# A two-layer float32 decoder trunk on one core: a re-priced instruction plan, float32r attention values, the last residual in halves, and ten matmuls on zeros ahead of TensorE's queue

## The chip, the cores and the metric

The kernel runs on one core of a Trainium2 chip. A core has TensorE (matmul, with a separate row for its weight loads), VectorE (DVE in the profile), ScalarE (ACT), GpSimd (POOL), and SyncE (SP), whose queue issues the DMA transfers here. The engines run their own queues in order and wait for each other by semaphores. The metric is the device time of one execution in microseconds (us), as the median of several runs.

## The reference

The input is 256 tokens of width 2048, in float32. Layer 0 mixes the tokens in two ways at once, with one input projection: sliding-window attention (16 query heads of 64, 2 key and value heads, blocks of 128 tokens, a learned sink for each head) and a gated delta rule (8 heads of 128). Layer 1 is a gated position mixing. Each layer ends with a SwiGLU feed-forward part of width 5632, and all residuals are added in float32.

```python
def reference(x, ...):
    h = x
    for i in range(DEPTH):
        j = i // 2
        if i % 2 == 0:
            h = h + even_mixer(rms_norm(h, even_norm[j]), ...)
        else:
            h = h + odd_mixer(rms_norm(h, odd_norm[j]), ...)
        h = h + swiglu(rms_norm(h, ffn_norm[i]), ...)
    return rms_norm(h, final_norm)
```

Inside the attention, for each block of 128 queries: scores against the block's own and the previous block's keys, a softmax with the sink, and then `einsum('bnhgqk,bnkhd->bnqhgd', p / denom, vb)`. The last product is what is called the value matmuls below.

## The kernel before

**Tiling.** The 256 tokens are two tiles of 128 rows (index t). A dense product runs over chunks of 512 output columns; `dense` (line 488) takes the input in blocks of 128 rows for each chunk. A weight tile `raw` holds four such blocks and comes by one DMA (1 MB, or 544 KB for the first chunk, which is only 272 wide). ScalarE casts each block to float32r (`whi`), VectorE subtracts to get the rest (`wlo`), and TensorE does three float32r matmuls for each token tile: activation-high by weight-high, activation-high by weight-low, activation-low by weight-high. There are three `raw` tiles, six `whi`, six `wlo` and four output banks `mm`. Activations are held as such high and low pairs in `unit` tiles, of which there are 58. `split` (line 446) makes a pair: a copy on ScalarE that casts, and a subtraction on VectorE.

**The first chunk.** `run` (line 1056) loads x in eight pieces `h` (four column chunks by two token tiles). `fill_unit` (line 452) transposes a piece on TensorE (four transposes into a `side` bank), multiplies by the norm's gain on VectorE, and splits. `chunk_stats` squares the piece on ScalarE with a running sum (its output goes to `junk`). The first product is the chunk "kvg" of the even mixer: keys, values and gates. The next is "qa0", the queries of the first eight heads.

**Small products.** Products other than the dense ones go to `side` banks: transposes, the delta rule's small products in float32 (a float32 matmul is two records in the profile), and products with the constant tiles `same` (line 723, `delta_inverse`) and `one` (line 587, `decay`) in float32r. In `delta_inverse`, each output is a pair of matmuls: the first operand is made by VectorE, the second by GpSimd.

**Attention.** `attention` (line 855) is called for two groups of heads and two token tiles. It transposes the probabilities (`tok_major`), copies each transposed block `pT` out on ScalarE, and multiplies by the values `va`: twelve float32 matmuls of 512 columns, each into one half of the output's rows. The result is split.

**The end.** `project` with `gain=None` writes the last dense product. In its last chunk `dense` holds back the second token tile's products by `LAG = 10`, so that the first tile finishes earlier. `residual` adds the product to `h`; then the square's sum, then h times the final gain `gf`. `finish` (line 1044) calls `end_norm` (a sum of four partial sums, a scale, and a power of -0.5 on GpSimd), scales the four pieces of a tile (three on VectorE, one on ScalarE) and writes them out.

**The order of work.** No instruction is issued as the program reads. Every operation is recorded (`Engine`, line 277 on) with a price in ns, a priority and its tile uses. `Schedule.plan` (line 190) then walks a clock: it takes at each step the engine that is free first and its ready operation of lowest priority number, gives it a tile if one is free, and sets its end by its price. `hop` (line 182) adds the way from engine to engine; to TensorE it is 1000 ns. The list sorted by planned start is the order in which each engine's queue is filled. A price in the table of `record` (lines 288 to 306) thus moves instructions everywhere, and on the chip the queues then keep that order whatever happens. In the profile all of them have line 179.

Of the kernel before, what the change touches and what calls it, by code (L numbers as in the profile page):

```python
# [16 lines left out]
P = 128  # L17
# [259 lines left out]
class Engine:  # L277
# [5 lines left out]
    def __getattr__(self, name):  # L283
        f = getattr(self.engine, name)

        def record(*args, **kw):
# [6 lines left out]
            elif k == "pe":  # L293
                cost = 3.0 + (107.0 if name == "transpose" else
                              (1.0 if aps[1].dtype == F32R and n >= 256 else 4.0) * n / 2.4)
# [6 lines left out]
            elif k == "dve":  # L302
                n = size(aps[1]) if name in ("tensor_reduce", "bn_stats") else n
                cost = (183.0 if name == "transpose" else 69.0) + (0.521 if name == "tensor_scalar" else 1.042) * n + 60.0 * scalars
            else:
                cost = 165.0 * n + 320.0 if ALU.pow in args else 1.9 * n + 200.0
# [9 lines left out]
class Trunk:  # L316
# [68 lines left out]
    def load_consts(self):  # L385
        nc, t = self.nc, self.t
        self.ident = self.keep((P, P), "ident")
        nc.sync.dma_start(self.ident, t["ident"])
        self.gains = self.const(t["gains"], [P, 4, 16], "gains")
        self.junk = self.keep((P, CW), "junk", BF16)  # L390
        self.mhalf = self.keep((P, 8), "mhalf")
        nc.vector.memset(self.mhalf, -0.5)
        self.phalf = self.keep((P, 8), "phalf")
        nc.vector.memset(self.phalf, 0.5)

# [134 lines left out]
    def project(self, w, units, gain, pcs=None):  # L530
# [3 lines left out]
        for n in range(NCH):  # L534
            self.residual(n, self.dense(w, units, n * size, pcs=pcs, lag=LAG if gain is None and n == NCH - 1 else 0))
            with self.prio(1):
# [7 lines left out]
                if gain is None:  # L544
                    for t in range(NT):
                        self.nc.vector.tensor_tensor(self.h[t][n], self.h[t][n], self.gf[n], ALU.mult)

# [286 lines left out]
    def attn_kv(self, ps):  # L834

        nc = self.nc
        self.va = self.small([P, NT, A_KV], "va")
        kk = self.unit(shape=(P, NT, 2, 2, 64))
        for t in range(NT):
# [3 lines left out]
            nc.scalar.activation(self.va[:, t], ps[t][:, A_KV:2 * A_KV], AF.Identity, scale=self.rstd[t])  # L843
        return kk

# [9 lines left out]
    def attention(self, kv, t, q, pair, kT):  # L855
# [35 lines left out]
        for s in ss:  # L891
            for b in range(nb):
                pT = self.unit()
                nc.scalar.copy(pT, self.tok_major(lambda m: s[:, m, b]))
                pTs.append(pT)
        out = self.side(P, 4, P)
        for r in range(2):
            rows = slice(64 * r, 64 * r + 64)
            for b, (own, kb) in enumerate(blocks):
                nc.tensor.matmul(out[rows].rearrange("p m i -> p (m i)"), self.va[:, kb, 64 * kv:64 * kv + 64],  # L900
                                 pTs[r * nb + b].rearrange("p m i -> p (m i)"), start=(b == 0), stop=(b == nb - 1))
# [142 lines left out]
    def finish(self):  # L1044
        nc = self.nc
        self.end_norm()
# [126 lines left out]
```

## Time and profile before

| | |
|---|---|
| time, median of 3 runs | 2168.47 us (2168.4 to 2168.81) |
| the profiled execution's own time | 2168.62 us |
| its span, first to last instruction | 2166.9 us |
| instructions | 27246 |
| mean granted TensorE clock | 0.999 |
| mean DMA rate | 184 GB/s, 399.08 MB moved |
| ACT table loads | 8 of 1283 ns |

The profiled execution's time is its span and 1.7 us around it. A row of a timeline gives the start of a group of like instructions from the span's start and how long it lasted, then the engine, the operation, what it writes and reads, the shape and the count; in brackets stands how long the engine had been idle and what ended that. `PEld` is TensorE's weight load, which overlaps its matmuls. A matmul's own length in the profile (some 390 ns at 512 columns) is longer than the distance to the next one's start, because matmuls are pipelined: distances of starts are what counts. In a table of windows, each row is a stretch of time with the busy time of each engine in the order of the head line, the granted clock, the DMA engines' share, and GB/s.

### The profile page before, as it was taken

How to read it: one execution, taken by the hardware profiler on the slowest of the kernel's cores; microseconds unless marked ns; L12 is line 12 of the kernel's file. 1: busy time of each engine (PE TensorE's matmuls, PEld its weight loads, DVE VectorE, ACT ScalarE, POOL GpSimd, SP SyncE). 2: the span in 40 equal slices, each digit the busy share in tenths (PEclk: the TensorE clock that was granted, in tenths of full speed). 3: DMA queues.
4: the chain of work that ended last, by engine and by line, in shares of the span. 5: the costliest groups of instructions: out<-in, count | busy, mean ns of one | idle time of the engine just before them, and what ended most of it. 6: DMA issues, size and time to landing. Idle time of an engine off the chain costs nothing.

```text
span 2166.9 us, 27246 instructions
## 1 busy us (share of the span) xinstructions
PE 2145.5 (99%) x9860; PEld 1774.7 (82%) x9860; DVE 1483.9 (68%) x2681; ACT 1133.6 (52%) x2034; POOL 55.7 (3%) x68
## 2 busy tenths in 40 slices
PE   8999999999999999999999999999999999999998
PEld 7788888888888888888888888888888888888886
DVE  7796786667766776657775576666677667755563
ACT  7665655554554555445545545555455544544453
POOL 1010110000000000000010000000000000000000
PEclk9999999999999999999999999999999999999999
DMA  7442434555555555556565555555555555555553
GB/s 246 136 156 79 156 117 156 194 179 193 194 195 194 192 194 194 194 194 201 204 231 184 194 171 178 189 188 192 193 190 194 194 193 194 195 202 194 194 199 131
DMA packets 58455, 399.08 MB, mean 184 GB/s; under 512 B 6976, under 2 KB 7232, under 8 KB 11216
## 3 DMA queue, kind: packets, MB, share of 16 engines
q1 hardware_dynamic: 57168, 393.61, 53.5%
q0 software_dynamic: 1152, 3.74, 0.6%
q8 instruction: 77, 1.26, 0.2%
q14 instruction: 58, 0.48, 0.1%
HBM read 395.22 MB, written 2.10 MB: 183 GB/s over the span
## 4 chain that ended last, share of the span: by engine, by line
PE 96%; DVE 2%; DMA 1%; issue 1%; ACT 1%; SPq 0%; POOL 0%; POOLq 0%; DVEq 0%; ACTq 0%
PE mm L179 90%; PE side L179 5%; DVE unit L179 1%; DVE wlo L179 1%; DMA raw<-in_even_in 1%; DMA h<-in_x 0%; ACT junk L179 0%; ACT whi L179 0%; DVE uc L179 0%; SPq L179 0%; DVE yt L179 0%; DVE yr L179 0%; DVE h L179 0%; POOL unit L179 0%; ACT L179 0%
## 5 line engine op out<-in xcount | busy, mean ns | idle before, releaser
L179 PE MATMUL mm<-whi,unit 128*128 128x512 f32 (+1 forms) x5864 | 1822.2, 390 | 0.0
L179 DVE TENSOR_TENSOR wlo<-raw,whi 128x512 fp32r<-128x512 f32 (+1 forms) x1466 | 1009.6, 690 | 618.1 <-ACT whi L179 606.9
L179 ACT CAST whi<-raw 128x512 fp32r<-128x512 f32 (+1 forms) x1466 | 908.1, 621 | 910.9 <-DVE wlo L179 546.3
L179 PEld LDWEIGHTS mm<-whi,unit 128*128 128x128 f32 x5864 | 1098.2, 188 | 224.4 <-issue 2.3
L179 PE MATMUL mm<-wlo,unit 128*128 128x512 f32 (+1 forms) x2932 | 1140.4, 389 | 0.0
L179 PEld LDWEIGHTS mm<-wlo,unit 128*128 128x128 f32 x2932 | 551.2, 188 | 113.7 <-issue 2.6
L179 DVE STREAM_TRANSPOSE wide<-wide 32x256 f32<-32x256 f32 x320 | 139.4, 436 | 7.6
L179 PE MATMUL side<-unit,unit 128*128 128x128 f32 (+3 forms) x448 | 60.6, 285 | 0.0
L179 PEld LDWEIGHTS side<-unit,unit 128*128 128x128 f32 (+2 forms) x448 | 54.4, 182 | 5.6 <-issue 1.4
L179 DVE TENSOR_TENSOR unit<-unit,unit 128x512 fp32r<-128x512 f32 (+1 forms) x56 | 39.7, 714 | 1.0 <-ACT unit L179 0.3
L179 PE MATMUL mm<-unit,unit 128*128 128x512 f32 x132 | 35.9, 389 | 0.0
L179 ACT COPY unit<-side 128x512 f32<-128x512 f32 (+1 forms) x36 | 20.5, 586 | 25.1 <-PE side L179 25.0
L179 ACT CAST unit<-wide 128x512 fp32r<-128x512 f32 x40 | 24.8, 620 | 15.3 <-DVE wide L179 15.3
L179 DVE SCALAR_TENSOR_TENSOR unit<-side,conv,unit 128x255 f32<-128x255 f32 (+2 forms) x72 | 31.2, 474 | 2.4 <-ACT unit L179 2.4
L179 ACT ACTIVATE junk<-h 128x512 bf16<-128x512 f32 x40 | 25.1, 628 | 14.0 <-DVE h L179 8.4
L179 DVE SCALAR_TENSOR_TENSOR wide<-mm,rstd,wide 128x512 f32<-128x512 f32 x44 | 30.9, 743 | 0.0
L179 ACT ACTIVATE wide<-mm,rstd 128x512 f32<-128x512 f32 x44 | 30.2, 686 | 0.4
L179 DVE STREAM_TRANSPOSE unit<-h 32x128 f32<-32x128 f32 x96 | 29.0, 302 | 1.9
L179 DVE TENSOR_TENSOR h<-mm,h 128x512 f32<-128x512 f32 x40 | 25.8, 683 | 6.3 <-PE mm L179 6.3
L179 PE MATMUL side<-ident,unit 128*128 128x128 f32 x180 | 28.6, 273 | 0.4 <-DVE unit L179 0.4
L179 PEld LDWEIGHTS mm<-unit,unit 128*128 128x128 f32 x132 | 24.8, 188 | 5.1
L179 POOL DMA_DIRECT2D unit<-in_final_g x4 | 2.4, 612 | 1015.4 <-PE mm L179 1014.6
(125 smaller groups left out, 579.4 us busy)
## 6 DMA issues: line engine op xcount, KB each, us to landing
raw<-in_gate SPq DMA_DIRECT2D x88, 1024.0 KB, 4.8
raw<-in_up SPq DMA_DIRECT2D x88, 1024.0 KB, 4.8
raw<-in_down SPq DMA_DIRECT2D x88, 1024.0 KB, 4.9
raw<-in_even_in SPq DMA_DIRECT2D x40, 1024.0 KB, 4.9
raw<-in_odd_in SPq DMA_DIRECT2D x32, 1024.0 KB, 4.9
raw<-in_even_out SPq DMA_DIRECT2D x16, 1024.0 KB, 4.8
raw<-in_odd_out SPq DMA_DIRECT2D x16, 1024.0 KB, 4.8
raw<-in_even_in SPq DMA_DIRECT2D x4, 544.0 KB, 7.1
```

What stands on the lines that cost most here:

```text
L179: f(*map(real, args), **{k: real(a) for k, a in kw.items()})
```

## The change

There are four edits.

1. **Prices.** In the planner's table a float32r matmul of n columns costs (n + 32) / 2.4 ns instead of 3 + n / 2.4, a transpose 127 instead of 110, a float32 matmul 17 ns more, a bfloat16 one 427; GpSimd's powers cost 30 more and its other operations 230 more.
2. **Warm-up.** The first entries of TensorE's queue are ten 512-column bfloat16 matmuls on `junk`, which GpSimd sets to zero first. They write an `mm` bank that nobody reads.
3. **Attention values.** The values are split into a high and a low float32r part, each stored between blocks of zeros so that a slice of 128 columns puts a head's values in the left or right half and zeros in the other. The transposed probabilities are split as well. Instead of twelve float32 matmuls there are 36 float32r matmuls over the full 128 rows, three for each of the old ones, all accumulating in one group.
4. **The last residual.** `last_chunk` adds the last chunk's product in two halves, squares each half with its own sum, multiplies by the gain into a new tile meanwhile, and finishes the norm from the sum of the first three chunks (reduced and scaled ahead) and the two half sums. `finish` no longer calls `end_norm`.

```diff
-                cost = 3.0 + (107.0 if name == "transpose" else
-                              (1.0 if aps[1].dtype == F32R and n >= 256 else 4.0) * n / 2.4)
+                one = aps[1].dtype == F32R and n >= 256
+                cost = (127.0 if name == "transpose" else (n + 32) / 2.4 if one else
+                        427.0 if aps[1].dtype == BF16 else 20.0 + 4.0 * n / 2.4)
...
-                cost = 165.0 * n + 320.0 if ALU.pow in args else 1.9 * n + 200.0
+                cost = 165.0 * n + 350.0 if ALU.pow in args else 1.9 * n + 430.0
...
+        self.warm_up()
...
+    def warm_up(self):
+
+        nc = self.nc
+        with self.prio(-40):
+            nc.gpsimd.memset(self.junk, 0.0)
+            ps = self.bank()
+            for _ in range(10):
+                nc.tensor.matmul(ps, self.junk[:, :P], self.junk, start=True, stop=True)
...
-            self.residual(n, self.dense(w, units, n * size, pcs=pcs, lag=LAG if gain is None and n == NCH - 1 else 0))
+            if gain is None and n == NCH - 1:
+                self.last_chunk(n, self.dense(w, units, n * size, pcs=pcs, lag=LAG))
+                break
+            self.residual(n, self.dense(w, units, n * size, pcs=pcs))
...
+    def last_chunk(self, n, ps):
...
+            for t in range(NT):
+                a = self.small([P, 1], "a")
+                nc.vector.tensor_reduce(a, self.ss[t][:, :n], AX.X, ALU.add)
+                nc.vector.tensor_scalar(a, a, 1.0 / D, EPS, ALU.mult, ALU.add)
+                h, o = self.h[t][n], self.unit(shape=(P, CW))
+                cs = [slice(i * half, (i + 1) * half) for i in range(2)]
+                sq = self.small([P, 2], "sq")
+                for i, c in enumerate(cs):
+                    nc.vector.tensor_tensor(h[:, c], ps[t][:, c], h[:, c], ALU.add)
+                    nc.scalar.activation(self.junk[:, c], h[:, c], AF.Square, accum_out=sq[:, i:i + 1])
+                nc.vector.tensor_tensor(o, h, self.gf[n], ALU.mult)
+                for i in range(2):
+                    b = self.small([P, 1], "b")
+                    nc.vector.tensor_scalar(b, sq[:, i:i + 1], 1.0 / D, a, ALU.mult, ALU.add)
+                    a = b
+                r = self.small([P, 1], "rstd")
+                nc.gpsimd.tensor_tensor(r, a, self.mhalf[:, 0:1], ALU.pow)
+                self.rstd.append(r)
+                self.h[t][n] = o
...
-        self.va = self.small([P, NT, A_KV], "va")
+        self.va = [self.new_values() for _ in range(NT)]
...
+            hi, lo = [x[:, :, 64:P] for x in self.va[t]]
+            nc.scalar.copy(hi, v)
+            nc.vector.tensor_tensor(lo, v, hi.bitcast(F32), ALU.subtract)
...
+    def new_values(self):
+
+        pair = [self.unit(F32R, (P, 2, 192)) for _ in range(2)]
+        for x in pair:
+            for o in (0, P):
+                self.nc.gpsimd.memset(x[:, :, o:o + 64].bitcast(F32), 0.0)
+        return pair
...
-                pT = self.unit()
-                nc.scalar.copy(pT, self.tok_major(lambda m: s[:, m, b]))
-                pTs.append(pT)
+                pT = [self.unit(F32R), self.unit(F32R)]
+                self.split(self.tok_major(lambda m: s[:, m, b]), pT)
+                pTs.append([x.rearrange("p m i -> p (m i)") for x in pT])
...
-                nc.tensor.matmul(out[rows].rearrange("p m i -> p (m i)"), self.va[:, kb, 64 * kv:64 * kv + 64],
-                                 pTs[r * nb + b].rearrange("p m i -> p (m i)"), start=(b == 0), stop=(b == nb - 1))
+                (vh, vl), (ph, pl) = [x[:, kv, cols] for x in self.va[kb]], pTs[r * nb + b]
+                first, last = r == 0 and b == 0, r == 1 and b == nb - 1
+                flat = out.rearrange("p m i -> p (m i)")
+                nc.tensor.matmul(flat, vh, ph, start=first, stop=False)
+                nc.tensor.matmul(flat, vh, pl, start=False, stop=False)
+                nc.tensor.matmul(flat, vl, ph, start=False, stop=last)
...
-        self.end_norm()
```

The order moves in many places; three of them matter below. In the names, `whi_...<-raw_...` is a cast of the first weight tile, `junk,ss<-h` a square of a piece of x, `unit<-unit` the high part of a transposed piece. ScalarE's queue at the start of the program, before:

```order
L179 ACT_TABLE_LOAD
L179 ACTIVATE junk_0_68_4472,ss_0_68_4471<-h_0_4_4444 128x512
L179 ACTIVATE junk_0_68_4472,ss_0_69_4481<-h_0_5_4446 128x512
L179 CAST unit_11_4485<-unit_10_4474 128x512
L179 CAST unit_18_4487<-unit_17_4483 128x512
L179 CAST whi_77_4491<-raw_76_4448 128x272
L179 CAST whi_85_4497<-raw_76_4448 128x272
L179 CAST whi_93_4502<-raw_76_4448 128x272
L179 CAST whi_101_4508<-raw_76_4448 128x272
```

And now:

```order
L179 ACT_TABLE_LOAD
L179 CAST whi_88_4513<-raw_87_4472 128x272
L179 CAST whi_96_4515<-raw_87_4472 128x272
L179 CAST whi_104_4524<-raw_87_4472 128x272
L179 CAST whi_112_4532<-raw_87_4472 128x272
L179 ACTIVATE junk_0_2_4460,ss_0_79_4538<-h_0_15_4468 128x512
L179 ACTIVATE junk_0_2_4460,ss_0_80_4550<-h_0_16_4470 128x512
L179 ACTIVATE junk_0_2_4460,ss_0_79_4538<-h_0_31_4474 128x512
L179 CAST whi_121_4578<-raw_120_4478 128x272
L179 CAST whi_129_4582<-raw_120_4478 128x272
L179 CAST unit_22_4589<-unit_21_4548 128x512
```

The casts of the first weight tile moved from behind the first two squares and the first two high parts to the head of the queue; three squares and two casts of the second weight tile now stand ahead of the first high part. VectorE's queue has the four subtractions of that tile first in the same way. On SyncE's queue the fourth weight tile's DMA moved ahead of the four constant tables. TensorE's queue at the same place, where `side<-ident,h` is four transposes of one piece of x and `mm` the first chunk's banks, before:

```order
L179 MATMUL side_6_4466<-ident_0_0_4438,h_0_4_4444 128x128 x4
L179 MATMUL side_13_4476<-ident_0_0_4438,h_0_5_4446 128x128 x4
L179 MATMUL side_22_4495<-ident_0_0_4438,h_0_20_4450 128x128 x4
L179 MATMUL side_29_4506<-ident_0_0_4438,h_0_21_4452 128x128 x4
L179 MATMUL mm_79_4516<-whi_77_4491,unit_11_4485 128x272
L179 MATMUL mm_82_4518<-whi_77_4491,unit_18_4487 128x272
L179 MATMUL mm_79_4516<-wlo_78_4504,unit_11_4485 128x272
```

And now, behind the ten matmuls on zeros and the transposes of the first three pieces of each token tile:

```order
L179 MATMUL side_49_4580<-ident_0_0_4462,h_0_47_4480 128x128 x4
L179 MATMUL side_56_4593<-ident_0_0_4462,h_0_48_4482 128x128 x4
L179 MATMUL mm_90_4606<-whi_88_4513,unit_22_4589 128x272
L179 MATMUL mm_90_4606<-wlo_89_4519,unit_22_4589 128x272
L179 MATMUL mm_93_4613<-whi_88_4513,unit_29_4596 128x272
L179 MATMUL mm_93_4613<-wlo_89_4519,unit_29_4596 128x272
L179 MATMUL side_65_4619<-ident_0_0_4462,h_0_63_4486 128x128 x4
L179 MATMUL mm_90_4606<-whi_88_4513,unit_23_4604 128x272
L179 MATMUL mm_90_4606<-whi_96_4515,unit_22_4589 128x272
L179 MATMUL side_72_4630<-ident_0_0_4462,h_0_64_4488 128x128 x4
L179 MATMUL mm_93_4613<-whi_88_4513,unit_30_4611 128x272
```

Three pairs of transposes instead of two stand ahead of the first matmul, and the last pair now comes after four and six of the 96 matmuls of this chunk, where it came after 27 and 29. TensorE's queue at the last two pairs of `same` matmuls of a `delta_inverse`, about a sixteenth of the way through the program, before:

```order
L179 MATMUL side_1232_5997<-unit_1230_5970,same_0_226_4670 128x512
L179 MATMUL side_1232_5997<-unit_1233_5960,same_0_226_4670 128x512
L179 MATMUL mm_869_5732<-wlo_955_5862,unit_50_4634 128x512
L179 MATMUL mm_869_5732<-whi_954_5854,unit_51_4652 128x512
L179 MATMUL mm_866_5722<-whi_963_5877,unit_59_4688 128x512
L179 MATMUL mm_866_5722<-wlo_964_5885,unit_59_4688 128x512
L179 MATMUL mm_866_5722<-whi_963_5877,unit_60_4704 128x512
L179 MATMUL mm_869_5732<-whi_963_5877,unit_66_4740 128x512
L179 MATMUL mm_869_5732<-wlo_964_5885,unit_66_4740 128x512
L179 MATMUL mm_869_5732<-whi_963_5877,unit_67_4747 128x512
L179 MATMUL side_1239_6023<-unit_1237_5992,same_0_226_4670 128x512
L179 MATMUL side_1239_6023<-unit_1240_5978,same_0_226_4670 128x512
```

And now:

```order
L179 MATMUL side_1273_6035<-unit_1271_5966,same_0_249_4713 128x512
L179 MATMUL side_1273_6035<-unit_1274_5964,same_0_249_4713 128x512
L179 MATMUL mm_907_5809<-wlo_972_5904,unit_54_4657 128x512
L179 MATMUL mm_907_5809<-whi_971_5892,unit_55_4681 128x512
L179 MATMUL mm_910_5822<-whi_971_5892,unit_61_4672 128x512
L179 MATMUL mm_910_5822<-wlo_972_5904,unit_61_4672 128x512
L179 MATMUL mm_910_5822<-whi_971_5892,unit_62_4699 128x512
L179 MATMUL side_1280_6053<-unit_1278_6021,same_0_249_4713 128x512
L179 MATMUL mm_907_5809<-whi_979_5908,unit_54_4657 128x512
L179 MATMUL side_1280_6053<-unit_1281_6024,same_0_249_4713 128x512
```

Between the two pairs stand five matmuls where there were eight, and the last pair now has a matmul between its two.

More of the change, by code (lines that the diff above doesn't have):

```diff
@@ L546, in project @@
                         self.nc.vector.tensor_tensor(self.h[t][n], self.h[t][n], self.gf[n], ALU.mult)
+    def last_chunk(self, n, ps):
+        nc = self.nc
+        half = CW // 2
+        self.rstd = []
+        with self.prio(1):
+            for t in range(NT):
[17 more added lines that the diff above has]
+                self.h[t][n] = o
     def gate_columns(self, ps):
@@ L842, in attn_kv @@
                 nc.scalar.activation(kk[:, t, :, r], src, AF.Identity, scale=self.rstd[t])
-            nc.scalar.activation(self.va[:, t], ps[t][:, A_KV:2 * A_KV], AF.Identity, scale=self.rstd[t])
-        return kk
+            v = self.unit(shape=(P, 2, 64))
+            nc.scalar.activation(v, ps[t][:, A_KV:2 * A_KV].rearrange("p (g d) -> p g d", g=2), AF.Identity,
+                                 scale=self.rstd[t])
+            hi, lo = [x[:, :, 64:P] for x in self.va[t]]
+            nc.scalar.copy(hi, v)
+            nc.vector.tensor_tensor(lo, v, hi.bitcast(F32), ALU.subtract)
+        return kk
+    def new_values(self):
[4 more added lines that the diff above has]
+        return pair
     def attn_keys(self, kk):
@@ L892, in attention @@
             for b in range(nb):
-                pT = self.unit()
-                nc.scalar.copy(pT, self.tok_major(lambda m: s[:, m, b]))
-                pTs.append(pT)
+                pT = [self.unit(F32R), self.unit(F32R)]
+                self.split(self.tok_major(lambda m: s[:, m, b]), pT)
+                pTs.append([x.rearrange("p m i -> p (m i)") for x in pT])
         out = self.side(P, 4, P)
         for r in range(2):
-            rows = slice(64 * r, 64 * r + 64)
+            cols = slice(64 - 64 * r, 192 - 64 * r)
             for b, (own, kb) in enumerate(blocks):
-                nc.tensor.matmul(out[rows].rearrange("p m i -> p (m i)"), self.va[:, kb, 64 * kv:64 * kv + 64],
-                                 pTs[r * nb + b].rearrange("p m i -> p (m i)"), start=(b == 0), stop=(b == nb - 1))
+                (vh, vl), (ph, pl) = [x[:, kv, cols] for x in self.va[kb]], pTs[r * nb + b]
[4 more added lines that the diff above has]
+                nc.tensor.matmul(flat, vl, ph, start=False, stop=last)
         self.split(out, pair)
```

## The prediction

> **What bounds the kernel now.** I read the page's busy times first, then what TensorE waits for, then the timelines of the first 28 us and the last 10 us.
>
> ```profile
> PE 2145.5 (99%) x9860; PEld 1774.7 (82%) x9860; DVE 1483.9 (68%) x2681; ACT 1133.6 (52%) x2034; POOL 55.7 (3%) x68
> ...
> PE side L179 <- DMA h<-in_x: 8.1, 2, 7.4
> PE side L179 <- DVE unit L179: 3.3, 4, 1.5
> ```
>
> The first row says that TensorE is busy for 99% of the span. The others say where its queue stood still: 8.1 us before the input arrives, and only 3.3 us for VectorE in the whole middle, 1.5 of it at one place. So there are three places from which time can come: the head, TensorE's own work, and the tail after its last matmul. The head, engine by engine (start, length in us):
>
> ```profile
> 2.59 0.43 SPq L179 DMA_DIRECT2D raw<-in_even_in  x1
> 7.33 0.63 ACT L179 ACTIVATE junk<-h 128x512 bf16<-128x512 f32 x1 [5.31 <-DMA h<-in_x]
> 7.45 1.94 PE L179 MATMUL side<-ident,h 128*128 128x128 f32 x8 [7.45 <-DMA h<-in_x]
> 7.98 1.70 SPq L179 DMA_DIRECT2D h<-in_x  x2
> 8.57 0.69 DVE L179 TENSOR_TENSOR unit<-side,gains 128x512 f32<-128x512 f32 x1 [7.66 <-PE side L179]
> 10.06 1.97 PE L179 MATMUL side<-ident,h 128*128 128x128 f32 x8 [0.67 <-DMA h<-in_x]
> 10.67 1.37 ACT L179 CAST whi<-raw 128x272 fp32r<-128x272 f32 x4
> 11.68 0.80 PE L179 MATMUL mm<-whi,unit 128*128 128x272 f32 x2
> 14.32 0.43 PE L179 MATMUL mm<-whi,unit 128*128 128x272 f32 x1
> 14.54 1.04 PE L179 MATMUL side<-ident,h 128*128 128x128 f32 x4
> 15.68 0.60 PE L179 MATMUL side<-ident,h 128*128 128x128 f32 x4
> 25.25 0.55 PE L179 MATMUL mm<-whi,unit 128*128 128x272 f32 x3
> 27.14 0.52 PE L179 MATMUL mm<-whi,unit 128*128 128x272 f32 x2
> ```
>
> Four transposes take 1.04 us at 14.54 and 0.60 us at 15.68: the clock doubles between the two, about 3.8 us after the first matmul (11.68). A 272-wide matmul starts 0.22 us after the one before while cold (14.32 to 14.54) and every 0.13 us later ((0.55 - 0.28) / 2 at 25.25). The second matmul of the row at 27.14, at 27.27, is the first of the next chunk (qa0): the 96 matmuls of the first chunk are done there.
>
> **The attention values.** A timeline around one of the twelve value matmuls, one around a pair, and six ordinary float32r matmuls:
>
> ```profile
> 74.86 0.63 PE L179 MATMUL mm<-whi,unit 128*128 128x512 f32 x2
> 75.42 1.07 PE L179 MATMUL side<-unit,va 128*64 128x512 f32 x2
> 76.43 0.50 PE L179 MATMUL mm<-wlo,unit 128*128 128x512 f32 x1
> 76.76 0.63 PE L179 MATMUL mm<-whi,unit 128*128 128x512 f32 x2
> ...
> 82.84 1.93 PE L179 MATMUL side<-unit,va 128*64 128x512 f32 x4
> ...
> 2149.66 1.52 PE L179 MATMUL mm<-unit,unit 128*128 128x512 f32 x6
> ```
>
> A float32 value matmul is two records. The second mm of the first row starts at 75.10 and the mm after the group's first at 76.76: 1.66 us, of which two ordinary matmuls are 2 x 0.226 ((1.52 - 0.39) / 5), so the group costs 1.21. A further matmul in a group adds (1.93 - 1.07) = 0.87. Four groups of one and four of two make 4 x 1.21 + 4 x 2.08 = 13.2; after their neighbouring transposes are taken out I count 12.9. In place stand 36 float32r matmuls x 0.226 = 8.1. TensorE gains **4.8 us**; bounds 4.0 (if some still pay for the changes around them) and 5.2. The Trainium skill, "TensorE: Matmul & The Clock Gate", section "Back-to-back issue gap", gives N / 2.4 + 2.5 ns for a warm matmul, 216 ns at 512 columns, measured on bf16; the row here shows 226, and by the page the gain would be 5.2.
>
> The new work elsewhere is twelve subtractions on VectorE (copies become casts of the same length), and a few 128-wide steps in the value projection:
>
> ```profile
> L179 DVE TENSOR_TENSOR unit<-side,unit 128x512 fp32r<-128x512 f32 (+1 forms) x24 | 16.5, 689 | 7.5 <-ACT unit L179 6.8 <-PE side L179 0.5
> ...
> 50.00:100.00 50.00, 50.00 (x252) 37.55 (x251) 36.74 (x88) 35.02 (x91) 0.00 (x0) 1.00 0.39 133
> 250.00:300.00 50.00, 48.78 (x242) 40.09 (x241) 48.40 (x142) 33.67 (x80) 9.13 (x10) 1.00 0.47 161
> ```
>
> 12 x 0.69 = 8.3 us. The first attention lies in the 50 to 100 us window, where VectorE (third busy time, 36.74 of 50) has 13 us free, so I cost it at nothing; 250 to 300, where it has 1.6 us free, is the delta rule's.
>
> **The tail.**
>
> ```profile
> 2157.14 0.84 PE L179 MATMUL mm<-unit,unit 128*128 128x512 f32 x3
> 2158.02 0.69 DVE L179 TENSOR_TENSOR h<-mm,h 128x512 f32<-128x512 f32 x1 [3.09 <-PE mm L179]
> 2158.80 0.63 ACT L179 ACTIVATE junk<-h 128x512 bf16<-128x512 f32 x1 [4.43 <-DVE h L179]
> 2159.34 0.19 ACT L179 ACTIVATION_READ_ACCUMULATOR junk<-h 128x1 f32 x1
> 2159.56 0.69 DVE L179 TENSOR_TENSOR h<-h,unit 128x512 f32<-128x512 f32 x1 [0.85 <-ACT junk L179]
> 2160.17 0.15 DVE L179 TENSOR_REDUCE tot<-ss 128x1 f32<-128x4 f32 x1
> 2160.35 0.15 DVE L179 TENSOR_SCALAR rstda<-tot 128x1 f32<-128x1 f32 x1
> 2160.59 0.55 POOL L179 TENSOR_TENSOR rstd<-rstda,mhalf 128x1 f32<-128x1 f32 x1 [6.97 <-DVE rstda L179]
> 2161.17 0.72 ACT L179 ACTIVATE unit<-h,rstd 128x512 f32<-128x512 f32 x1 [1.64 <-POOL rstd L179]
> ```
>
> From the last matmul's end (2157.98) to the first scaling are 3.19 us. After the change: two half adds, about 0.4 each with the second issued 0.35 after the first (half of 0.69), so the halves of h stand at +0.46 and +0.80. ScalarE squares the first from +0.55, the second from +1.10, and its sum is out at +1.62. VectorE multiplies by the gain meanwhile (+0.83 to +1.5), then two 0.15 steps to +1.80, the power from +1.89 to +2.44, scaling at +2.47. **0.7 us** gained (0.4 to 0.9); the eight output transfers keep their order.
>
> **The head.** Ten 512-wide matmuls at 0.42 (0.22 x 512 / 272) are 4.2 us. They wait for a memset on POOL, of a length that no row here shows; even at 1.5 us they would end by 6.6, before the input at 7.33, and I take 6: no cost of their own. The nine memsets on POOL stand ahead of one transfer that is needed only at the end. But the new order costs. ScalarE's queue now begins with the four casts of the first weight tile, and VectorE's with their four subtractions. Landings (us from issue) of that tile and of the last two pieces of x:
>
> ```profile
> raw<-in_even_in SPq DMA_DIRECT2D x1, 544.0 KB, 6.7
> ...
> h<-in_x SPq DMA_DIRECT2D x1, 256.0 KB, 7.4
> ...
> h<-in_x SPq DMA_DIRECT2D x1, 256.0 KB, 6.8
> ```
>
> The tile lands at 2.59 + 6.7 = 9.3, so ScalarE begins 2 us later than at 7.33 and VectorE at about 9.8, not 8.57. ScalarE: casts to 10.6, three squares of 0.73 (as in the tail, 2158.80 to 2159.53) to 12.8, two casts, then the first piece's cast ends at 14.0, and the first matmul starts at 14.1, not 11.68. After four matmuls TensorE's queue holds the transposes of the last pieces of x, landing at 7.98 + 7.4 = 15.4 and 9.35 + 6.8 = 16.1; 90 of the 96 matmuls stand behind the second. At full clock they end at 16.1 + 0.45 + 90 x 0.127 = 28.0, against 27.27: 0.7 us late, warm-up and all. VectorE's queue is done by 26.5, so it does not set this.
>
> At half clock it is worse, and I think it will be half. When the clock falls:
>
> ```profile
> 2157.98:2162.40 4.42, 0.00 (x1) 1.00 0.00 0
> 2162.50:2166.90 4.40, 0.00 (x0) 0.50 0.64 238
> ```
>
> After the window and its length stand TensorE's busy time with its count and then the granted clock: it is halved 4.5 us after the last matmul. Between the zeros (end near 6) and the first matmul (14.1) are 8 us with nothing but transposes, and in the trace 3.9 us of transposes (1.94 from 7.45 and 1.97 from 10.06) did not raise the clock, which rose 3.8 us after the first matmul. So transposes seem not to count. The Trainium skill agrees: "TensorE: Matmul & The Clock Gate", "Part 4: PE-mode transpose", says that a transpose isn't counted as TensorE being busy in the way of a matmul. Cold, the two groups of transposes take 0.85 each, and the last starts at 16.8 and ends at 17.65; with the clock back some 3.3 us later, at 20.9, 14.5 of the 90 matmuls are done and 75.5 x 0.127 = 9.6 follow: 30.5, **3.2 us** later than before. Bounds 2.4 (clock back at 19) and 4.3 (at 23).
>
> **The joins in the middle.** The order changes everywhere in the even mixer. One of the stalls:
>
> ```profile
> 139.74 0.73 PE L179 MATMUL side<-unit,same 128*128 128x512 f32 x2 [0.69 <-DVE unit L179]
> ```
>
> Here TensorE waits for a VectorE product. With GpSimd's products priced higher, the second matmul of such a pair now stands one to three matmuls behind the first in three pairs of four, and runs of float32 work between float32r matmuls fall from 129 to 108 (counted in the order); both should save. But this pair has five matmuls ahead of it where it had eight, the stall of 1.5 us keeps its order, and the plan's TensorE, 5% too fast before (0.216 for 0.226), hid slack that is now gone. I take **-0.8 us**, between -3.0 (nearly all of the 3.3 gone) and +3 (two more like the 1.5).
>
> **Sum.** -4.8 - 0.7 + 3.2 - 0.8 = -3.1 against the profiled execution's 2168.62 (span 2166.9 and 1.7 around it, 0.15 above the median of the runs): **2165.4 us** against the median.
>
> **Rivals.**
> *The clock stays up.* If transposes count for keeping the clock, it holds: the first start 1.4 us after the zeros (7.45) and others follow at 10.06 and later, so no gap comes near 4.5 us, and the head costs 0.7: -5.6, 2162.9. For it: the short gaps. Against: the cold transposes above. The Trainium skill, "TensorE: Matmul & The Clock Gate", "Why this matters for your kernels", asks only for no idle gap over some 3 us between bursts, and by that rule it would come out so.
> *Slower.* The value matmuls now wait in TensorE's queue for a cast and a subtraction each. If each of the twelve lows comes one subtraction late, 12 x 0.7 = 8.4: +5.3, 2173.8. It makes the kernel slower by more than 4.3 from 0.62 us each. Against: eight matmuls and four transposes (2.3 us) stand between a piece's transposes and its first use, for a cast of 0.6 and a subtraction of 0.7.
> *Other joins are worse* than the bound of +3, by stalls like the two above at places that the order does not show: +4 to +6 over the forecast, 2169 to 2171.
>
> **Chances.** Forecast 0.57, clock up 0.28, slower 0.05, other joins 0.10. A measurement of this kernel tells about 0.2% (4.3 us) from no change. The forecast is beyond it when the joins are better by 1.2, three times in ten (0.18), the second case nearly always (0.24): faster 0.42. Slower are the third case and a few of the last: 0.07. The rest, 0.51, is the same. The range goes from the second case with joins 1.3 better, 2161.6, to the forecast with joins 3.4 worse, 2168.8, and leaves out about a tenth at each end.
>
> **What would show it.** First matmul near 14 and qa0 near 30.5 (28 with the clock up); 36 value matmuls 0.226 apart with no wait; scaling 2.5 us after the last matmul. An earlier qa0 than 27.3, or over 6 us of new waits in the middle, would prove it wrong.

## The result, and the profile after

| | before | after |
|---|---|---|
| median time | 2168.57 us (2168.28 to 2168.81, 10 runs) | 2174.06 us (2172.23 to 2174.89, 10 runs) |
| profiled execution | 2168.62 us, span 2166.9 | 2174.04 us, span 2172.0 |
| first dense matmul, first of qa0 | 11.68, 27.27 us | 16.02, 30.66 us |
| end of the last matmul to the first scaling | 3.19 us | 2.63 us |

The change makes the kernel slower: ratio 1.0025, 95% interval 1.0017 to 1.0033. The forecast was 3.1 us faster, with a range up to 2168.8.

The span grew by 5.1 us. I split it by comparing the start of the n-th dense matmul in the two traces: it is 3.4 us late at qa0 and 5.74 us late at the last one, and the tail gives 0.6 back. The 2.3 us that come in between hold 4.5 saved on the value matmuls, so 6.8 are lost at the joins. What TensorE waited for, after (us in total, times, longest):

```profile
PE side L179 <- DMA h<-in_x: 5.7, 2, 4.9
PE side L179 <- POOL unit L179: 5.4, 4, 1.6
PE side L179 <- DVE unit L179: 4.2, 4, 1.9
PE mm L179 <- POOL junk L179: 1.3, 1, 1.3
PE side L179 <- ACT whi L179: 0.5, 2, 0.3
```

The second row did not exist before: four waits for GpSimd, in a program where GpSimd is busy for 3% of the time. The first of them in the timeline, TensorE, then GpSimd, then VectorE:

```profile
120.53 0.63 PE L179 MATMUL mm<-whi,unit 128*128 128x512 f32 x2
122.80 0.50 PE L179 MATMUL side<-unit,same 128*128 128x512 f32 x1 [1.64 <-POOL unit L179]
...
118.68 3.49 POOL L179 TENSOR_TENSOR unit<-ucp,unit 128x256 fp32r<-128x256 f32 x1 [7.78 <-PE mm L179]
...
118.80 0.68 DVE L179 TENSOR_TENSOR wlo<-raw,whi 128x512 fp32r<-128x512 f32 x1
119.40 1.08 DVE L179 TENSOR_TENSOR unit<-ucp,unit 128x256 fp32r<-128x256 f32 x3
120.41 0.68 DVE L179 TENSOR_TENSOR wlo<-raw,whi 128x512 fp32r<-128x512 f32 x1
121.01 0.68 DVE L179 TENSOR_TENSOR unit<-unit,unit 128x512 f32<-128x512 f32 x1
121.73 1.01 DVE L179 TENSOR_REDUCE uc<-unit 128x64 f32<-128x512 f32 x1
```

GpSimd's product starts at 118.68 and ends at 122.17, 3.49 us, where the next one takes 0.61. Meanwhile VectorE issues one operation after the other whose two inputs both lie in tiles (none in a `side` or `mm` bank), until 121.69; "two-input operations" below means these; then comes a reduction, with one input, and GpSimd is done 0.48 us later. The same product before:

```profile
118.60 1.96 POOL L179 TENSOR_TENSOR unit<-ucp,unit 128x256 fp32r<-128x256 f32 x1 [8.78 <-PE mm L179]
...
119.33 0.74 DVE L179 TENSOR_TENSOR unit<-ucp,unit 128x256 fp32r<-128x256 f32 x2
120.29 1.26 DVE L179 SCALAR_TENSOR_TENSOR unit<-side,conv,unit 128x255 f32<-128x255 f32 x3 [0.22 <-ACT unit L179]
```

VectorE's run ends at 120.07 there, and what follows reads one input from a `side` bank. GpSimd ends at 120.56, again 0.48 to 0.49 later. So both times GpSimd's product gets its turn only when VectorE's run of two-input operations ends, and the new order put it at the start of a longer run.

The head after, with TensorE's and ScalarE's rows and then the clock (window and its length, TensorE's busy time and count, four more engines, granted clock, DMA share, GB/s):

```profile
1.32 4.45 PE L179 MATMUL mm<-junk 128*128 128x512 bf16 x10 [1.32 <-POOL junk L179]
5.56 1.20 PE L179 MATMUL side<-ident,h 128*128 128x128 f32 x8
10.92 1.38 ACT L179 CAST whi<-raw 128x272 fp32r<-128x272 f32 x4 [8.90 <-DMA raw<-in_even_in]
11.63 1.97 PE L179 MATMUL side<-ident,h 128*128 128x128 f32 x8 [4.87 <-DMA h<-in_x]
16.02 0.58 PE L179 MATMUL mm<-whi,unit 128*128 128x272 f32 x1
30.54 0.52 PE L179 MATMUL mm<-whi,unit 128*128 128x272 f32 x2
```

```profile
5.90:9.30 3.40, 0.86 (x8) 0.62 (x6) 0.00 (x0) 0.00 (x0) 0.00 (x0) 1.00 0.61 199
9.40:19.40 10.00, 6.95 (x31) 6.50 (x32) 7.92 (x16) 8.32 (x23) 0.00 (x0) 0.50 1.03 392
19.60:30.00 10.40, 10.40 (x85) 10.40 (x84) 9.26 (x26) 8.32 (x24) 3.07 (x2) 1.00 0.77 252
```

The zeros raise the clock for one window of 3.4 us, in which there are only transposes; then it is halved, from 9.3 to 19.5 us. That it would be halved was forecast. The first pieces of x are there by 5.56 us, 1.9 us earlier than before, and the first weight tile only near 10.9, where the landing time of before gave 9.3. Why the transfers moved was not followed; the transfer of the final gain starts at 2.34 here and at 1.26 before. Two groups of value matmuls (36 in all), and the tail:

```profile
85.99 1.55 PE L179 MATMUL side<-unit,unit 128*128 128x512 f32 x6
87.84 1.30 PE L179 MATMUL side<-unit,unit 128*128 128x512 f32 x5
...
2162.88 0.84 PE L179 MATMUL mm<-unit,unit 128*128 128x512 f32 x3
2163.76 0.76 DVE L179 TENSOR_TENSOR h<-mm,h 128x256 f32<-128x256 f32 x2 [3.60 <-PE mm L179]
2164.69 0.40 ACT L179 ACTIVATE junk<-h 128x256 bf16<-128x256 f32 x1
2165.47 0.21 DVE L179 TENSOR_SCALAR b<-sq,b 128x1 f32<-128x1 f32 x1
2165.76 0.55 POOL L179 TENSOR_TENSOR rstd<-b,mhalf 128x1 f32<-128x1 f32 x1 [6.92 <-DVE b L179]
2166.35 0.72 ACT L179 ACTIVATE unit<-h,rstd 128x512 f32<-128x512 f32 x1 [1.16 <-POOL rstd L179]
```

The value matmuls start (1.55 - 0.39) / 5 = 0.23 us apart and wait for nothing inside a group; all 36 take 8.45 us from start to start. The old twelve took 11.5 by the same count, and 12.9 with the matmuls and transposes at their edges, which were some 0.1 us longer there and are not now. From the last matmul's end (2163.72) to the scaling are 2.63 us.

### The profile page after: what moved, and what is told of

It reads as the page before. It is cut to its first block, busy times and chain, and to the rows that moved or that the text cites. A ratio compares the mean times of both kernels' runs of the same rounds, so it can differ in the third digit from the quotient of the medians.

```text
span 2172.0 us, 27290 instructions
## 1 busy us (share of the span) xinstructions
PE 2146.3 (99%) x9882; PEld 1778.5 (82%) x9882; DVE 1486.8 (68%) x2701; ACT 1134.2 (52%) x2040; POOL 66.1 (3%) x77
## 3 DMA queue, kind: packets, MB, share of 16 engines
q8 instruction: 77, 1.26, 0.2%
## 4 chain that ended last, share of the span: by engine, by line
PE 93%; DVE 4%; ACT 1%; issue 1%; POOL 1%; DMA 0%; SPq 0%; POOLq 0%; DVEq 0%; ACTq 0%
PE mm L179 88%; PE side L179 4%; DVE wlo L179 1%; DVE unit L179 1%; ACT whi L179 1%; DMA h<-in_x 0%; POOL unit L179 0%; DVE wide L179 0%; ACT wide L179 0%; ACT unit L179 0%; SPq L179 0%; DVE mx L179 0%; POOL rq L179 0%; ACT junk L179 0%; DVE den L179 0%
## 5 line engine op out<-in xcount | busy, mean ns | idle before, releaser
L179 PE MATMUL side<-unit,unit 128*128 128x128 f32 (+4 forms) x484 | 70.6, 293 | 0.1
L179 PEld LDWEIGHTS side<-unit,unit 128*128 128x128 f32 (+2 forms) x484 | 59.8, 182 | 8.0 <-DVE unit L179 1.8
L179 DVE TENSOR_TENSOR unit<-unit,unit 128x512 fp32r<-128x512 f32 (+2 forms) x58 | 39.3, 687 | 0.3 <-ACT unit L179 0.3
L179 DVE SCALAR_TENSOR_TENSOR unit<-side,conv,unit 128x254 f32<-128x254 f32 (+2 forms) x72 | 29.9, 473 | 3.9 <-ACT unit L179 3.9
L179 PE MATMUL side<-ident,unit 128*128 128x128 f32 x180 | 28.4, 274 | 2.3 <-DVE unit L179 1.8
L179 DVE TENSOR_TENSOR h<-mm,h 128x512 f32<-128x512 f32 (+1 forms) x42 | 25.9, 657 | 6.8 <-PE mm L179 6.8
L179 ACT ACTIVATE junk<-h 128x512 bf16<-128x512 f32 (+1 forms) x42 | 25.6, 609 | 9.1 <-DVE h L179 8.4
L179 PEld LDWEIGHTS side<-ident,unit 128*128 128x128 f32 x180 | 21.7, 140 | 9.9 <-issue 2.1
```

The lines of the kernel that those rows point to most:

```text
L179: f(*map(real, args), **{k: real(a) for k, a in kw.items()})
```

## The experiments

Sixteen kernels ran. Each time is a median; the kernel before gave 2168.4 to 2168.7 beside them, and ratios are against it. "Stalls" below are the distances between starts on TensorE, from 30 to 430 us, that exceed the usual distance of their kind by over 0.3 us, added up: 5.1 us before, 12.1 after.

### Each edit alone

The prices alone:

```diff
-                cost = 3.0 + (107.0 if name == "transpose" else
...
+                cost = (127.0 if name == "transpose" else (n + 32) / 2.4 if one else
...
+                cost = 165.0 * n + 350.0 if ALU.pow in args else 1.9 * n + 430.0
```

> The kernel before with the new prices alone. Of the 5.1 us by which the span grew, the dense matmuls show +3.4 by the first matmul of qa0, +2.3 between there and the last one (with 4.5 saved on the value matmuls, so 6.8 lost at the joins), and -0.6 behind. Theory 1, the prices lose the joins: 6 to 7 us of new waits in the middle here too, at the products with 'same' that wait for GpSimd (four stalls over 1 us each), 2174 to 2176 us. Theory 2, the instructions that the value edit adds lose them: 2168 to 2169.5. Theory 3, any new plan moves the joins by a few us in either direction: 2166 to 2172, with stalls at other places than in the changed kernel.

**2173.91 us**, ratio 1.0028 (1.0016 to 1.0039). Theory 1 holds, 0.1 us under its range. Its waits for GpSimd are those of the changed kernel:

```profile
PE side L179 <- POOL unit L179: 5.4, 4, 1.6
PE side L179 <- DVE unit L179: 3.2, 3, 1.5
```

Stalls are 10.6 us, with the same sizes in the same order (1.81, 1.24, 1.80, 1.23, 1.62). The dense matmuls lose 5.0 us between qa0 and 400 us.

The values alone (the diffs of `attn_kv`, `new_values` and `attention`):

```diff
+        self.va = [self.new_values() for _ in range(NT)]
...
+                nc.tensor.matmul(flat, vh, ph, start=first, stop=False)
+                nc.tensor.matmul(flat, vh, pl, start=False, stop=False)
+                nc.tensor.matmul(flat, vl, ph, start=False, stop=last)
```

> The kernel before with the attention values alone. Theory 1 (the prices lose the joins): 4.5 us saved and joins as before, 2164 us (2163.3 to 2165). Theory 2 (the added instructions lose them): 2168.6 - 4.5 + 6.8 = 2170.9. Theory 3 (any new plan): 2162 to 2168 with stalls at other places.

**2165.76 us**, ratio 0.9987 (0.9979 to 0.9996): faster by 2.75, but not by 4.5. One new stall of 2.22 us stands at an inverse, at 116.7, and right behind it the granted clock is halved for 3.4 us, which costs TensorE half of that, 1.7 us. The half clock is a loss that none of the three theories had. But the time and the new place of the stall are what theory 3 allows, so that a new order by itself can cost some us is not excluded by this run: the stall is a GpSimd product of 4.09 us, at the old prices.

The zeros alone:

```diff
+        self.warm_up()
```

> The kernel before with the ten matmuls on zeros alone. The first matmul of qa0 came 3.4 us later in the changed kernel. Theory A, the zeros alone do that (their price in the plan moves the squares of x behind the first weight casts, and the clock falls again before the first matmul): qa0 at 30.3 to 31, 2171.5 to 2172.5 us, with the clock up at about 5.9, down one window of 3.4 us later, and up again past 19. Theory B, the head needs the eight other memsets on GpSimd or the new prices to be late (the transfer of the final gain behind them collides with the first weights): qa0 by 29, 2168.5 to 2170.5.

**2173.05 us**, ratio 1.0021 (1.0012 to 1.0030), 0.5 us above theory A's range. The 97th dense matmul, which is the first of qa0 in the kernel before, comes at 31.24. (In this order the first of qa0 stands earlier, at 28.9, ahead of the last twelve of the first chunk.) Theory A in kind: the transfer of the final gain is issued at 1.28 here, as before, and the head is late all the same.

The last residual alone:

```diff
+                self.last_chunk(n, self.dense(w, units, n * size, pcs=pcs, lag=LAG))
...
-        self.end_norm()
```

> The kernel before with the last residual by halves alone. The order ahead of the last chunk stays as it was. Last matmul as before, first scaling 2.6 us behind its end instead of 3.2: 2167.8 to 2168.1 us. If the halves did nothing by themselves (the 0.6 of the changed kernel came from elsewhere): 2168.6.

**2167.92 us**, ratio 0.9997 (0.9988 to 1.0006): the 0.6 us of the expectation, though by itself within the measurement's uncertainty.

### All but the prices

```diff
-                cost = (127.0 if name == "transpose" else (n + 32) / 2.4 if one else
...
+                cost = 3.0 + (107.0 if name == "transpose" else
```

> The changed kernel with the old prices: zeros, values and halves stay. If the three edits and the prices add up (values alone -2.75, zeros alone +4.5, halves alone -0.6): 2168.5 + 1.2 = 2169.7 us (2168.7 to 2170.7), with the stalls of 1.81, 1.24 and 1.62 us of the price run gone. If the losses at the joins come with any new plan: 2172 to 2175, with such stalls at other places.

**2170.02 us**, ratio 1.0006 (0.9998 to 1.0015): the edits add up within 0.3 us. Stalls are 6.5 us; those at the second group's inverse and at 336 are gone, and one of 1.95 at the first inverse stays, which the values alone have too (2.22).

### Who makes the product

The plan and every queue's order are kept, and only the call is changed after it is recorded:

```diff
+                    op = self.schedule.ops[-1]
+                    op.call = (nc.vector.engine.tensor_tensor, *op.call[1:])
```

> The changed kernel in its own planned order, with one difference: the 16 products of 128x256 that GpSimd makes for the low parts of the inverse are issued on VectorE, at the place in time where the plan had them on GpSimd. On GpSimd the first of a row took 3.26 to 3.49 us in the trace, four times, while VectorE ran operations with two inputs from on-chip memory back to back; one beside nothing took 0.61. Theory P (GpSimd and VectorE exclude each other): the four waits of TensorE for GpSimd (1.81, 1.23, 1.81, 1.23) go, each product costs VectorE 0.41: 2168.0 to 2170.5 us. Theory Q (the plan's order is too tight there for whichever engine makes the products, as VectorE is full): the waits turn into waits for VectorE of the same size, 2173 to 2176 us.

**2172.27 us**, between the two theories. The waits for GpSimd are gone:

```profile
PE side L179 <- DVE unit L179: 6.8, 9, 1.9
PE side L179 <- ACT unit L179: 1.3, 2, 0.7
PE side L179 <- DVE yr L179: 0.7, 2, 0.4
```

But the sixteen products lengthen VectorE's queue, and smaller waits for it stand at joins behind (0.82, 0.64 and 0.89 us, twice each). Stalls fall only from 12.1 to 10.9. So these four waits are GpSimd's, as theory P says, and the order has little room for the work on the other engine either, as theory Q says.

### Which price

GpSimd's alone, and TensorE's alone (the two halves of the first diff):

> The kernel before with GpSimd's new prices alone (products 0.92 for 0.69 us in the plan). In its order the first pair of an inverse has three matmuls between its products and the second pair still stands some 40 instructions behind. If GpSimd's price alone lost the joins: 2173 to 2175 us, with GpSimd products over 3 us. If it is TensorE's price, which brings the second pair to 7 instructions behind the first: within 1 us of the kernel before, 2167.5 to 2169.5.

**2167.47 us**, ratio 0.9996 (0.9988 to 1.0005).

> The kernel before with TensorE's new prices alone. In its order the second pair of an inverse stands close behind the first, as with both prices. If TensorE's price loses the joins: GpSimd products over 3 us and stalls over 1 us at the same places as with both prices, 2172.5 to 2175. If it needs GpSimd's price too: 2167 to 2169.5.

**2177.26 us**, ratio 1.0037 (1.0024 to 1.0051): TensorE's price it is, and alone it is worse than with GpSimd's, 2.3 us above the forecast range. In this trace the stalls at 118.2 and 258.5 are 2.24 us long, where the changed kernel has 1.81, and both times the clock falls; the sum of the stalls, 10.9 us, is hardly more than the 10.6 of both prices, so the 3.4 us between the two times are about these two half-clock windows (an estimate: half of 3.4 us, twice). Three neighbouring windows around the first (columns as above):

```profile
118.45:121.80 3.35, 1.25 (x7) 0.80 (x6) 2.26 (x4) 0.45 (x1) 3.35 (x4) 1.00 0.63 264
121.90:125.20 3.30, 3.30 (x11) 2.77 (x10) 2.67 (x6) 2.50 (x7) 0.01 (x1) 0.50 0.02 5
125.30:128.60 3.30, 3.30 (x16) 2.72 (x15) 2.20 (x5) 2.18 (x6) 0.00 (x0) 1.00 0.25 37
```

TensorE is busy for 1.25 of 3.35 us in the first, and runs at half clock in the second, 11 matmuls for 16. In the trace of the zeros alone a window with 1.61 of 3.30 us, around a stall of 2.07, leaves the clock as it is:

```profile
43.35:46.65 3.30, 1.61 (x7) 1.38 (x8) 3.30 (x9) 0.21 (x1) 1.46 (x2) 1.00 0.84 276
46.75:50.10 3.35, 3.35 (x16) 2.79 (x15) 3.35 (x15) 3.13 (x5) 0.00 (x0) 1.00 0.07 22
```

One number of the changed kernel put back:

```diff
-                cost = (127.0 if name == "transpose" else (n + 32) / 2.4 if one else
+                cost = (127.0 if name == "transpose" else 3.0 + n / 2.4 if one else
```

> The changed kernel with one number of the plan back: a float32r matmul of n columns is priced 3 + n / 2.4 ns again (216 for 512 columns) where the chip takes 226; all other new prices and all three edits stay. Theory S (the price of a dense matmul was the slack: each of them ahead of a join in the queue gave the other engines 10 ns more than the plan counted): second pairs of an inverse stand some 40 instructions behind the first again, the stalls of 1.81, 1.23 and 1.62 us go, 2168 to 2170.5 us. Rival (the prices of transposes, float32 matmuls or GpSimd matter as much): 2172 to 2175.

**2166.38 us**, ratio 0.9989 (0.9980 to 0.9998): 7.7 us faster than the changed kernel, faster than theory S had it, for 10 ns in a price that the chip never sees. Stalls are 4.8 us. Not all of it lies at the joins: the 97th dense matmul is at 28.4, 2.3 us earlier than in the changed kernel, so the price moves the head as well, which theory S left out. (The trace is that of the fastest of eleven executions, which lie between 2164.12 and 2167.33.)

Slack added elsewhere:

```diff
-        return 1000.0 if b.engine == "pe" else 200.0 if a.engine == "pe" else 130.0
+        return 2000.0 if b.engine == "pe" else 200.0 if a.engine == "pe" else 130.0
```

> The changed kernel with all its new prices, but the way from an engine to TensorE priced at 2000 ns in the plan instead of 1000. Theory S in its simple form (any slack ahead of TensorE's joins will do): the stalls of 1.81, 1.23 and 1.62 us shrink by up to 1 us each, sum of stalls over 0.3 us down from 12.1 to under 7, 2168 to 2171 us. Rival (it is where the products fall among VectorE's two-input operations that counts, and slack does not move that): GpSimd products over 3 us remain, stalls over 1 us remain, 2172 to 2176.

**2169.47 us**, stalls 6.5 us: inside theory S. Yet the rival is right on the trace: GpSimd's first products take 2.9 and 4.4 us here, 4.4 being the longest of all runs, and two stalls of 1.24 remain. So slack does not shorten the products; TensorE meets them later:

```profile
PE side L179 <- DVE unit L179: 2.9, 6, 0.8
PE side L179 <- POOL unit L179: 2.2, 2, 1.1
```

### The zeros without a price

```diff
+            for op in self.schedule.ops[-11:]:
+                op.cost = 0.0
```

> The kernel before with the ten matmuls on zeros alone, priced at nothing in the plan, so that every other instruction keeps the order of the kernel before; only the transfer of the final gain is issued half a us later. Theory A (the zeros cost through the order of the head, and the clock that they raise is lost again within one or two windows): first matmul at 11.4 to 11.8, qa0 within 0.7 us of 27.3, 2168.0 to 2169.0. Rival (the matmuls on zeros or their memset cost by themselves): qa0 past 28.5, over 2169.5. Rival (the raised clock pays once the order is kept): qa0 under 26.5, under 2167.8.

**2168.87 us**, ratio 1.0001 (0.9993 to 1.0010), first matmul at 12.11, qa0 at 27.91. Theory A in the main: with the order of the head kept, the zeros neither cost nor bring anything that the time shows, and the clock is down again from 9.1 to 16.0. One thing was not kept: ScalarE's table load of 1.28 us comes at 7.83 here, behind its wait for x, and at 0.74 before, so its first square starts 1.8 us later (9.13 for 7.33) and the first matmul 0.4 us later. Some tenths of a us that the zeros might bring can be hidden by that.

### A faster version, and a sweep of the price

Values and halves alone, which is the second and the fourth diff above together:

> The two edits that paid alone, values and halves, with the old prices and without the zeros. If they add up: 2168.5 - 2.75 - 0.6 = 2165.1 us (2164.3 to 2166). With the stall of 2.22 us at an inverse in the values run, the clock fell for one window of 3.41 us; where that falls otherwise, 1.7 us less: 2163.4.

**2165.60 us**, ratio 0.9987 (0.9978 to 0.9996), with the stall of 2.22 us, its GpSimd product of 4.09 and the halved window again. Then the changed kernel without its zeros, at four prices of a dense matmul in the plan:

```diff
-        self.warm_up()
...
-                cost = (127.0 if name == "transpose" else (n + 32) / 2.4 if one else
+                cost = (127.0 if name == "transpose" else (n - 16) / 2.4 if one else
```

> The changed kernel without its zeros, a 512-column float32r matmul priced 207 ns in the plan (the chip takes 226). Theory S (a price under the true one is slack, and the loss grows with the price): as fast as at 216 or faster, 2163 to 2165 us, no GpSimd product over 2.5 us. Theory L (chance: any change of the plan's numbers gives another order, good or bad): anywhere from 2162 to 2171, with no order among the four prices.

> The changed kernel without its zeros, priced 216 ns. With the zeros it took 2166.4, and its first matmul of qa0 came 1.15 us later than in the kernel before. Theory S: 2166.4 less 1.2 to 2, so 2164.4 to 2165.2 us, the fastest so far. Theory L: 2162 to 2171.

> The changed kernel without its zeros, priced 222 ns. In its order the second pair of an inverse stands 34 to 37 instructions behind the first (41 at 216, 7 at 226). Theory S: between its neighbours, 2165 to 2168.5 us. Theory L: 2162 to 2171.

> The changed kernel without its zeros, with all its prices (226 ns). The zeros alone cost 4.5 us on the kernel before, and 3.4 us by the first matmul of qa0 in the changed kernel. If that is theirs here too: 2174.1 - 3.4 to 4.5 = 2169.6 to 2170.7 us, with the stalls of 1.81, 1.23 and 1.62 us in place. If the zeros cost nothing together with the other edits: 2173.5.

| price of 512 columns, ns | time, us | ratio | stalls, us | longest GpSimd product, us | second pair behind the first |
|---|---|---|---|---|---|
| 207, n - 16 | 2163.81 | 0.9978 (0.9969 to 0.9987) | 5.4 | 1.13 | 61, 10 |
| 216, 3 + n / 2.4 | 2163.62 | 0.9977 (0.9968 to 0.9986) | 5.2 | 1.95 | 59, 61 |
| 222, n + 20 | 2167.61 | 0.9995 (0.9986 to 1.0003) | 8.5 | 4.31 | 57, 57 |
| 227, n + 32 | 2170.28 | 1.0010 (1.0001 to 1.0018) | 11.8 | 3.49 | 7, 7 |

The last column counts TensorE's matmul records from the end of an inverse's first pair to the start of its second, in the traces, for the two groups of heads (63 and 63 in the kernel before). At 222 it is the third pair that has moved up, from 25 and 24 records behind the second to 13 and 13, and the product of 4.31 us is its. In the run of the values alone the first group's second pair stands 8 behind, at the old prices, and the stall of 2.22 us is in that group. The 10 in the first row comes without a long product: the column says what goes with what, not what causes it.

The times rise with the price, as theory S has it, and the two low prices are alike. The step from 207 to 216 is no gain, so this is a margin that is used up above 216, not a line. Four points don't exclude that a fifth falls out of line, and how the plan gets from a price to an order was not followed. The last row also gives the zeros' share in the changed kernel: 2174.06 - 2170.28 = 3.8 us. That figure is rough, for the eleven executions of the last row lie between 2168.74 and 2172.40, the five above 2172 at a mean granted clock of 0.998 and the others at 0.999.

At 216 the kernel is 5.1 us faster than before and 10.4 faster than the changed one. Its waits:

```profile
PE side L179 <- DMA h<-in_x: 7.7, 3, 4.6
PE side L179 <- DVE unit L179: 4.2, 6, 1.2
PE side L179 <- ACT unit L179: 0.2, 1, 0.2
```

No wait for GpSimd is left, and none for VectorE is over 1.2 us.

## Why the prediction was wrong, point by point

**The joins: the step that failed.** The prediction took them at -0.8 us, between -3.0 and +3; they cost 6.8. The forecast said that the plan's TensorE, 5% too fast, hid slack that is now gone, and then let the better spacing of pairs outweigh it. The price put back alone and the sweep show that this slack is the main thing: at 227 ns the plan puts an inverse's second pair 7 matmul records behind its first, at 216 some 60, and the long products and stalls come with that order. Why is argued and not shown: with the true 226 ns every other price in the plan has to be true as well, and GpSimd's is not one number. Its product takes 0.61 us alone and 3.49 us at the head of a run of VectorE's two-input operations; the new price of 0.92 fits neither. The row of 1.96 us beside rows of 0.61 stood in the trace of before, and the sum did not use it. "Over 6 us of new waits in the middle" was named there as what would prove the forecast wrong, and stalls grew by 7.0. The rival "other joins are worse" had the kind and the direction, at 0.10 and 4 to 6 us; it, too, was short: 2169 to 2171. The old price is no full protection either, as the values alone show with a stall of 2.22 us.

**The head: right in size, by two errors that cancel.** Forecast +3.2 and qa0 near 30.5; measured +3.4 and 30.66. The first matmul came at 16.0, not 14.1, as the first weight tile was cast from 10.9 and not 9.3, and the clock was back at 19.5, not 20.9. That the clock would not hold was right, so "the clock stays up" did not happen. The reason given, that transposes don't count, is not shown by this fall: TensorE was busy for 0.86 us of the 3.40 ahead of it, less than in any window of the middle after which the clock fell, whatever the kind of the matmuls. That the weights would land later, and x earlier, was in no term of the sum. The zeros alone and the unpriced zeros show that the order made the head late.

**The values: right.** Forecast -4.8, measured -4.5 (the 5.2 given there for 216 ns should be 5.1: 12.9 less 36 x 0.216), with starts 0.23 us apart, no wait inside a group, and the casts and subtractions hidden. "Slower", in which each of the twelve lows comes late, did not happen.

**The tail: right.** Forecast -0.7 with scaling 2.47 us behind the last matmul; measured -0.6 and 2.63, since a one-column step with a column as its scalar takes 0.21 and not 0.15 us.

With the joins as they were, the sum is -4.5 + 3.4 - 0.6 = -1.7: the sign came from that one term.

## What to carry to other kernels

In a list scheduler a price is not only an estimate of a duration. Where other costs are left out (two engines that shut each other out, a wait that depends on what runs beside it), a price that is too low on the bound engine can be the margin for them, as here, and correcting it alone takes the margin away. Before re-pricing an operation, look at the spread of its durations in the trace, not at the mean: two values far apart mean that it waits for something, and no one price can carry that. Matmuls on zeros brought nothing here, since the clock that they raised was lost again after one window, in which TensorE had only transposes, for 0.86 of 3.40 us; whether more zeros, up to the first real matmul, would pay was not tried. And a stall of TensorE of some 2.2 us can cost nearly 4, with the half-clock window behind it.

## What the runs showed of the hardware

**GpSimd can have to wait for the end of VectorE's run, not only for one operation.** GpSimd makes 272 of the 128x256 products in the eighteen traces (16 in each but one), and 42 of them took over 1.5 us, up to 4.42. All of these ended 0.47 to 0.49 us after the last operation of an unbroken run on VectorE (3 to 14 two-input operations, each starting as the one before ends). The Trainium skill, "SBUF — State Buffer", "SBUF: two separate sides", states the rule: GpSimd and such VectorE operations share one pair of ports, and whichever has it keeps it for the whole instruction. The rows agree, and the 42 show in addition that a waiting GpSimd may be passed over at every change from one of VectorE's instructions to the next. It is not always so. In 101 other products GpSimd got in at the end of the operation that ran when it started, though the next stood right behind, and that next one was longer instead. In the kernel before, where such operations of 128x56 and 128x256 take 0.20 and 0.41 us alone:

```profile
136.32 0.68 DVE L179 TENSOR_TENSOR wlo<-raw,whi 128x512 fp32r<-128x512 f32 x1
136.93 0.63 DVE L179 TENSOR_TENSOR yr<-yr,yt 128x56 f32<-128x56 f32 x1
137.48 0.87 DVE L179 TENSOR_TENSOR unit<-ucp,unit 128x256 fp32r<-128x256 f32 x1
...
136.41 2.99 POOL L179 TENSOR_TENSOR unit<-ucp,unit 128x256 fp32r<-128x256 f32 x4 [2.54 <-DVE yt L179]
```

What decides between the two is open. VectorE waits in longer operations too: beside a GpSimd product of 128x512 VectorE's subtraction takes 1.77 us where its mean is 0.69 (in the changed kernel, ahead of the stall of 1.62 us at 336):

```profile
335.69 1.77 DVE L179 TENSOR_TENSOR wlo<-raw,whi 128x512 fp32r<-128x512 f32 x1
...
333.68 3.23 POOL L179 TENSOR_TENSOR unit<-unit,rows 128x512 f32<-128x512 f32 x2
```

**The clock falls in the middle of dense work after a stall of some 2.2 us.** The clock's changes stand a whole number of 3.4133 us apart in each trace (2146.98 = 629 of them, before); such a stretch is called a window here. In the middle of the program it fell after six windows, in which TensorE's recorded busy share was 0.37 to 0.44, around stalls of 2.08 to 2.24 us; it held after all others of the stretch from the first dense matmuls to 420 us, of which the lowest had 0.48. Each fall lasted one window and cost about half of it, 1.7 us. So a stall of 2.1 us may or may not cost the clock, by where it lies in a window (2.08 did in the kernel with the old prices, 2.28 in that with the price of 222 did not). The Trainium skill, "TensorE: Matmul & The Clock Gate", "Why this matters for your kernels", warns of idle gaps over some 3 us; here 2.1 to 2.2 were enough, so the measurement decides.
